# Output projection of a gated-parallel layer by Strassen's method: seven half-size products in place of eight

## The chip, the cores and the metric

One core of one Trainium2 chip runs the whole kernel. The metric is the device time of one execution in microseconds (us), the median over several runs; a profile is one further execution, recorded by the hardware profiler.

## The reference, cut to what matters

One layer over 1024 latent tokens of width 1024, with 256 context tokens: a modulated RMSNorm, one wide input projection, two branches (gated linear attention and differential attention), a gated merge, an output projection, a gate and a residual. The change touches the last three lines.

```python
def combine(o_gla, gla_gate, o_diff, diff_gate, m_gla, m_diff,
            gla_gain, diff_gain, lam_init, w_br_gla, w_br_diff, w_out):
    a = merge_heads(rms_norm(o_gla) * gla_gain) * jax.nn.silu(gla_gate)
    b = merge_heads(rms_norm(o_diff) * diff_gain * (1 - lam_init)) * jax.nn.silu(diff_gate)
    y = jax.nn.sigmoid(m_gla) * (a @ w_br_gla) + jax.nn.sigmoid(m_diff) * (b @ w_br_diff)
    return y @ w_out
...
        x = x + g_x * out_x
```

Everything is float32, y and w_out are 1024x1024.

## The kernel before, in words

All large products are done on TensorE (PE) in a split form: a float32 tensor is written as hi + lo, both in the type fp32r, and a product is three matmuls (hi by hi, hi by lo, lo by hi; `mm3`, L325). The split (`split`, L335) is a copy with rounding on ScalarE (ACT), hi, and a subtraction on VectorE (DVE), lo = source - hi. A half is thus ready when VectorE has written lo.

The order of every engine's instructions is written out when the program is built. Generators (`load`, `conv`, `half_tile`, `post_y` and so on) stand for strands of work; a `Driver` (L57) keeps a rough clock of each engine and resumes a strand when what it waits for is due by that clock. What a strand issues is appended to the queue of its engine, and on the chip each queue runs strictly in that order, waiting on semaphores for true dependences. `d.on("DVE", tile)` waits until the tile is due and the engine's queue is short; `acq` and `rel` count the buffers of a tag, and a strand that finds none waits. All DMAs go out from one queue, SP's (`dma`, L275), in the order in which they are issued.

The stages are: adaLN and input projection (phase A), both branches (phase B), and the merge and output (phase C). Beside the attention of phase B, `fill` (L1626) runs products that depend on little: gate products, the product with w_br_gla, and at the end that with w_br_diff (kind 2). For each of 8 column tiles `dt` of 128 channels and each `half` of 512 tokens, 8 x 3 matmuls make a PSUM tile `mc` [128 channels, 512 tokens]; `load_y` (L1814) brings the gate and the first branch, `post_y` (L1825) makes y on VectorE in two instructions (PSUM tile by gate, plus first branch), and splits y at once into the tag `yy`. y is thus kept transposed, channels on partitions. The right operands of `fill` sit in 32 buffers of the tag `h`, released half by half when the last product has read them.

`to_c` (L1848) opens phase C's pools and calls `wstream`, which loads w_out in 8 pieces of 512 KB (`raw`) and splits them into `h` buffers. `stream` (L1884) does the projection: for each of two column halves c of w_out and each of 8 tiles i of 128 tokens, 8 x 3 matmuls over the channel tiles k into one `mc` tile. `post_out` (L1874) finishes a tile in two VectorE instructions (PSUM tile by gate `gb`, plus x) and stores it. Four `o` buffers carry x in and the result out; `load_x` (L1867) fills them.

The seam is the moment at which PE goes from the last half-tile of y to the first tile of the projection.

## Time and profile before

| | |
|---|---|
| median of 3 runs | 1734.94 us (1734.45 to 1736.46) |
| the profiled execution: its own time | 1732.79 us |
| its span, first to last instruction | 1731.1 us |
| mean granted TensorE clock | 0.996 |
| PE busy, share of the span | 97% |
| DVE, ACT, POOL busy | 60%, 43%, 41% |

How to read the rows: PE is TensorE's matmuls and PEld its weight loads, DVE is VectorE, ACT is ScalarE, POOL is GpSimd, SP is the queue that issues the DMAs. A row of the timeline gives start and duration in us, the engine, the line of kernel.py, the operation, output<-inputs by the program's names without buffer numbers, the shapes, how many like instructions are merged (x4) and, in brackets, how long the engine had been idle and what ended that. Many operations are recorded under the line of a helper (L185 for ACT, DVE and POOL, L320 for matmuls, L285 for DMAs), so the tile names tell them apart. Rows of groups give busy time and the mean ns of one. Rows of stretches give, for a stretch in us from the span's start, the busy time of each engine with its number of instructions.

### The profile page before, as it was taken

What the parts mean: (1) busy time and instruction counts of PE and PEld (TensorE: products, weight loads), DVE (VectorE), ACT (ScalarE), POOL (GpSimd) and SP (SyncE); (2) the same over time, 40 slices, a digit from 0 to 9 for tenths busy, and PEclk for the clock granted to TensorE, in tenths of its full rate; (3) what the DMA queues carried; (4) which work ended last, traced back from release to release, by engine and by line L of the source; (5) the groups of instructions that cost most, each with busy time, mean ns of one, the idle gap of its engine ahead of it and who ended that gap; (6) DMA issues with size and microseconds to landing.
All of it is one profiled execution on the core that took longest, in us unless ns stands there. A gap on an engine that the chain in (4) does not pass through costs nothing.

```text
span 1731.1 us, 25030 instructions
## 1 busy us (share of the span) xinstructions
PE 1681.9 (97%) x8605; PEld 1398.8 (81%) x8605; DVE 1036.4 (60%) x1897; ACT 750.7 (43%) x1741; POOL 708.7 (41%) x917
## 2 busy tenths in 40 slices
PE   8999999999999999999999999999999999999998
PEld 3788788888888888888888777878878788888887
DVE  4534325525564767768653888778777787524532
ACT  4636422321343343344343666666666666522200
POOL 1500002404234345545430667777777787820000
PEclk9999999999999999999999999999999999999999
DMA  8423345453742646346345235335347652278322
GB/s 313 153 89 122 140 149 161 134 179 103 247 157 87 211 133 190 121 134 203 118 132 169 76 96 157 106 99 148 96 140 235 193 157 92 90 237 292 138 100 85
DMA packets 244751, 258.84 MB, mean 150 GB/s; under 512 B 20840, under 2 KB 176400, under 8 KB 244624
## 3 DMA queue, kind: packets, MB, share of 16 engines
q1 hardware_dynamic: 244624, 257.25, 47.2%
q8 instruction: 68, 1.11, 0.3%
q14 instruction: 59, 0.48, 0.1%
HBM read 170.68 MB, written 86.51 MB: 149 GB/s over the span
## 4 chain that ended last, share of the span: by engine, by line
PE 87%; DVE 5%; DMA 2%; ACT 2%; issue 2%; POOL 2%; SPq 0%; ACTq 0%; DVEq 0%; POOLq 0%
PE mm L320 42%; PE mc L320 12%; PE mb L320 7%; PE b L320 6%; PE s L320 5%; PE b L332 3%; DVE sm L185 3%; PE go L320 3%; PE gs L320 2%; PE gt L320 2%; PE tp L332 2%; PE st L320 2%; POOL at L185 1%; DMA w<-in_w_ada 1%; DVE e L185 1%
## 5 line engine op out<-in xcount | busy, mean ns | idle before, releaser
L320 PE MATMUL mm<-w,h 128*128 128x512 f32 x2304 | 569.3, 399 | 1.4 <-DVE w L185 1.4
L320 PEld LDWEIGHTS mm<-w,h 128*128 128x128 f32 x2304 | 425.6, 188 | 87.5 <-DVE w L185 2.1
L185 POOL TENSOR_TENSOR at<-ac,at 128x512 fp32r<-128x512 f32 (+1 forms) x192 | 222.1, 1157 | 16.0
L320 PE MATMUL mb<-h,wt 128*128 128x512 f32 x792 | 218.1, 405 | 1.2 <-ACT ft L185 0.7
L185 POOL TENSOR_SCALAR at<-ac 128x512 fp32r<-128x512 f32 (+1 forms) x192 | 145.2, 756 | 143.1 <-ACT ac L185 131.1
L185 ACT ACTIVATE p<-mm 128x512 f32<-128x512 f32 (+1 forms) x116 | 67.5, 587 | 217.3 <-PE mm L320 197.6
L320 PEld LDWEIGHTS mb<-h,wt 128*128 128x128 f32 x792 | 138.8, 189 | 25.0 <-DVE ft L185 1.5
L185 DVE TENSOR_REDUCE sm<-s 128x1 f32<-128x1024 f32 x128 | 155.6, 1216 | 3.5 <-PE s L320 2.4
L185 ACT ACTIVATE ac<-b 128x512 f32<-128x512 f32 (+1 forms) x213 | 107.9, 508 | 103.4 <-PE b L332 82.7
L320 PE MATMUL mm<-h,w 128*128 128x512 f32 x576 | 143.3, 401 | 0.7 <-DVE h L185 0.6
L185 ACT ACTIVATE e<-s,sm 128x1024 f32<-128x1024 f32 x128 | 142.7, 1115 | 0.0
L320 PE MATMUL s<-kk,aq 128*128 128x512 f32 x512 | 134.9, 397 | 0.2 <-ACT p L185 0.2
L320 PE MATMUL b<-at,vv 128*128 128x256 f32 x960 | 131.8, 287 | 3.1 <-ACT ac L185 3.1
L185 POOL TENSOR_SCALAR sm<-sm 128x1 f32<-128x1 f32 (+1 forms) x78 | 16.9, 216 | 287.4 <-DVE sm L185 167.0
L320 PEld LDWEIGHTS b<-at,vv 128*128 128x128 f32 x960 | 124.1, 192 | 7.4 <-ACT ac L185 3.9
L320 PEld LDWEIGHTS mm<-h,w 128*128 128x128 f32 x576 | 107.9, 191 | 24.1 <-DVE h L185 1.6
L185 DVE TENSOR_TENSOR w<-raw,w 128x512 fp32r<-128x512 f32 x120 | 86.3, 736 | 64.4 <-ACT w L185 63.1
L332 PE MATMUL b<-ident,e 128*128 128x128 f32 x604 | 94.2, 275 | 23.8 <-ACT ac L185 12.7
L185 POOL TENSOR_TENSOR sm<-sm,nhalf 128x1 f32<-128x1 f32 (+2 forms) x110 | 107.2, 975 | 13.9 <-DVE sm L185 7.4
L332 PEld LDWEIGHTS b<-ident,e 128*128 128x128 f32 x604 | 71.5, 140 | 44.8 <-ACT ac L185 18.7
L320 PEld LDWEIGHTS s<-kk,aq 128*128 128x128 f32 x512 | 90.8, 190 | 14.8 <-ACT p L185 0.4
L185 DVE SCALAR_TENSOR_TENSOR e<-e,sm,e 128x1280 f32<-128x1280 f32 x64 | 101.7, 1589 | 0.2
(199 smaller groups left out, 2609.4 us busy)
## 6 DMA issues: line engine op xcount, KB each, us to landing
raw<-in_w_in SPq DMA_DIRECT2D x72, 512.0 KB, 4.2
aq<-d_qT SPq DMA_DIRECT2D x128, 128.0 KB, 3.1
d_kT<-pl SPq DMA_DIRECT2D x40, 256.0 KB, 2.3
d_dv<-pl SPq DMA_DIRECT2D x40, 256.0 KB, 2.6
kk<-d_kT SPq DMA_DIRECT2D x32, 320.0 KB, 5.3
gv<-d_v SPq DMA_DIRECT2D x40, 256.0 KB, 2.8
vv<-d_dv SPq DMA_DIRECT2D x16, 640.0 KB, 6.1
d_aT<-gpl SPq DMA_DIRECT2D x64, 128.0 KB, 1.9
```

The lines of the kernel that those rows point to most:

```text
L185: f(out, *args, **kw)
L320: self.nc.tensor.matmul(out, lhsT, rhs, start=start, stop=stop)
L332: self.nc.tensor.transpose(out, src, self.ident[:n, :n])
```

## The change

The projection y @ w_out is cut into 2 x 2 blocks of 512x512. With y11..y22 (token half, channel half) and w11..w22, Strassen's method in Winograd's form makes seven block products out of sums of blocks:

- left operands, in this order: y11, y12, s1 = y21 + y22, s2 = s1 - y11, s3 = y11 - y21, y22, s4 = y12 - s2
- right operands: w11, w21, t1 = w12 - w11, t2 = w22 - t1, t3 = w22 - w12, t4 = w21 - t2, w22
- the output blocks are sums of the products: block 11 is the first two (accumulated in one PSUM tile); block 22 is the first, third, fourth and fifth; block 21 is the first, fourth, fifth and sixth; block 12 is the first, third, fourth and seventh.

Each product is 4 token tiles x 4 channel tiles x 3 matmuls, so 48 matmuls; there are 336 in place of 384. `post_y` leaves y as float32 in the tag `yf`; `left` makes the sums s1 to s4 on POOL and `right` the differences t1 to t4 on VectorE, both in float32, and each operand is split afterwards (`operand`: hi on ACT, lo on VectorE). `right` loads w11 and w21 as before into `raw`, and all four blocks again as 16 tiles into the buffers `h1`. `stream` runs the seven products in order, four token tiles each; what has to be kept of a product is drained from PSUM into the buffers `wt` and `wx` (`after`). `finish` ends the blocks 11, 22 and 21: one VectorE instruction that reads PSUM, then on POOL the product with the gate (blocks 22 and 21) and the sum with x, then the store. For block 12, `with_x` prepares gate times the earlier products plus x on POOL, and `finish12` does two VectorE instructions and the store.

To make room, the tag `h` (32) is split in two, `h0` and `h1` (16 each), for the two token halves, `kk` gets a pool of its own that is closed when phase C opens, and there are three more PSUM tiles `mz`.

```diff
-        h=("sb", 32), raw=("sb", 3), gb=("sb", 1), sm=("sb", 32), kk=("sb", 3),
+        h0=("sb", 16), h1=("sb", 16), raw=("sb", 3), gb=("sb", 1), sm=("sb", 32), kk=("sbK", 3),
...
-        yy=("sbC", 32), o=("sbC", 4), wx=("sbC", 4),
+        yy=("sbC", 24), yf=("sbC", 16), sf=("sbC", 2), o=("sbC", 4), wx=("sbC", 4),
...
-        mb=("psW", 1), s2=("psB", 2), st=("psB1", 1), b1=("psB1", 2), mc=("psC", 4),
+        mb=("psW", 1), s2=("psB", 2), st=("psB1", 1), b1=("psB1", 2), mc=("psC", 4), mz=("psD", 3),
...
-    def mm(self, out, lhsT, rhs, start, stop):
-        self.nc.tensor.matmul(out, lhsT, rhs, start=start, stop=stop)
+    def mm(self, out, lhsT, rhs, start, stop, more=False):
+        self.nc.tensor.matmul(out, lhsT, rhs, start=start, stop=stop, skip_group_check=more)
...
-    def mm3(self, out, sh, sl, mh, ml, first, last):
-        self.mm(out, sh, mh, first, False)
-        self.mm(out, sh, ml, False, False)
-        return self.mm(out, sl, mh, False, last)
+    def mm3(self, out, sh, sl, mh, ml, first, last, more=False):
+        self.mm(out, sh, mh, first, False, more)
+        self.mm(out, sh, ml, False, False, more)
+        return self.mm(out, sl, mh, False, last, more)
...
-                yield from self.acq("h", 2)
+                yield from self.acq(f"h{half}", 2)
...
-            hi = self.t("hc" if ctx else "h", [P, n], F32R)
-            lo = self.t("hc" if ctx else "h", [P, n], F32R)
+            hi = self.t("hc" if ctx else f"h{half}", [P, n], F32R)
+            lo = self.t("hc" if ctx else f"h{half}", [P, n], F32R)
...
-                        yield from self.acq("h")
-                        tt = r[j][k][half] = self.t("h", [P, 512], F32R)
+                        yield from self.acq(f"h{half}")
+                        tt = r[j][k][half] = self.t(f"h{half}", [P, 512], F32R)
...
-                    self.rel("h", e, 2 * NK)
+                    self.rel(f"h{half}", e, 2 * NK)
...
-        self.dve.tensor_tensor(my[:, 0], my[:, 0], my[:, 1], ALU.add)
-        hi = self.t("yy", [P, 512], F32R)
-        lo = self.t("yy", [P, 512], F32R)
-        self.y[dt, half] = (hi, lo)
-        yield self.d.when(my)
-        e = yield from self.split(my[:, 0], hi, lo)
+        y = self.y[dt, half] = self.t("yf", [P, 512])
+        e = self.dve.tensor_tensor(y, my[:, 0], my[:, 1], ALU.add)
...
-            yield from self.idle("st", "b1", "e5", "b1k", "aq", "vv", "at4", "at2", "ac")
-            self.close("psB1", "sbB2", "sbB")
-            self.open("sbC")
+            yield from self.idle("st", "b1", "e5", "b1k", "aq", "kk", "vv", "at4", "at2", "ac")
+            self.close("psB1", "sbB2", "sbB", "sbK")
+            self.open("sbC", "psD")
...
-            wd = self.wstream([(wo, 0), (wo, 512)], "h")
+            d.spawn(left(), prio=-2)
+            d.spawn(right(), prio=-2)
...
-            d.spawn(stream(wd, self.gb), prio=9)
-        ev_x = {(c, i): Event() for c in range(2) for i in range(8)}
+            d.spawn(stream(), prio=9)
+        LEFT = ("y11", "y12", "s1", "s2", "s3", "y22", "s4")
+        RIGHT = ("w11", "w21", "t1", "t2", "t3", "t4", "w22")
+        ev_l, ev_r = ({(n, k): Event() for n in names for k in range(4)} for names in (LEFT, RIGHT))
+        def operand(ev, tag, src, then=()):
+            hi = self.t(tag, [P, 512], F32R)
+            lo = self.t(tag, [P, 512], F32R)
+            ev.w = (hi, lo)
+            def run():
+                yield d.on("ACT", src)
+                e = yield from self.split(src, hi, lo)
+                d.set(ev, e)
+                for f in then:
+                    f(e)
+            d.spawn(run(), prio=-2)
+        def left():
+            y = lambda r, c, k: self.y[4 * c + k, r]
+            ready = {"y11": ((0, 0),), "y12": ((0, 1),), "s1": ((1, 0), (1, 1))}
+            add = self.pool.tensor_tensor
+            for n in LEFT:
+                for k in range(4):
+                    for r, c in ready.get(n, ()):
+                        yield self.ev_y[4 * c + k, r]
+                    then = ()
+                    if n in ("s1", "s2"):
+                        yield from self.acq("sf")
+                        src = self.t("sf", [P, 512])
+                        yield d.on("POOL", y(1, 0, k), y(1, 1, k))
+                        if n == "s2":
+                            add(src, y(1, 1, k), y(0, 0, k), ALU.subtract)
+                            add(src, src, y(1, 0, k), ALU.add)
+                            add(y(0, 1, k), y(0, 1, k), src, ALU.subtract)
+                        else:
+                            add(src, y(1, 0, k), y(1, 1, k), ALU.add)
+                        then = [lambda e: self.rel("sf", e)]
+                    else:
+                        src = y(*{"y11": (0, 0), "y12": (0, 1), "s3": (1, 0), "y22": (1, 1), "s4": (0, 1)}[n], k)
+                    if n == "s3":
+                        yield d.on("POOL", src)
+                        add(src, y(0, 0, k), src, ALU.subtract)
+                    yield from self.acq("yy", 2)
+                    operand(ev_l[n, k], "yy", src, then)
+        def right():
+            for n, r in (("w11", 0), ("w21", 512)):
+                for kk in range(2):
+                    yield from self.acq("raw")
+                    raw = self.t("raw", [P, 2, 512])
+                    self.dma(raw, wo[r + kk * 256:r + kk * 256 + 256, 0:512].rearrange("(k p) c -> p k c", p=P))
+                    for j in range(2):
+                        yield from self.acq("h0", 2)
+                        operand(ev_r[n, 2 * kk + j], "h0", raw[:, j], [lambda e: self.rel("raw", e)] if j else ())
+            w = {}
+            for n in ("w11", "w12", "w22", "w21"):
+                for k in range(4):
+                    yield from self.acq("h1")
+                    x = w[n, k] = self.t("h1", [P, 512])
+                    r, c = (int(n[1]) - 1) * 512 + k * P, (int(n[2]) - 1) * 512
+                    self.dma(x, wo[r:r + P, c:c + 512])
+            for n, out, a, b, last in (("t1", "w11", "w12", "w11", None), ("t2", "w11", "w22", "w11", "t1"),
+                                       ("t3", "w12", "w22", "w12", None), ("t4", "w21", "w21", "w11", None),
+                                       ("w22", "w22", None, None, None)):
+                for k in range(4):
+                    if last:
+                        yield ev_r[last, k]
+                    if a:
+                        yield d.on("DVE", w[a, k], w[b, k])
+                        self.dve.tensor_tensor(w[out, k], w[a, k], w[b, k], ALU.subtract)
+                    if k % 2:
+                        for kk in (k - 1, k):
+                            yield from self.acq("h0", 2)
+                            operand(ev_r[n, kk], "h0", w[out, kk])
+        ev_w = [Event() for _ in range(4)]
+        ev_x = {(r, c, t): Event() for r, c in ((0, 0), (1, 1), (1, 0)) for t in range(4)}
         def load_x():
-            for c, i in ev_x:
+            for r, c, t in ev_x:
...
-                xo = ev_x[c, i].t_ = self.t("o", [P, 2, 512])
+                xo = ev_x[r, c, t].t_ = self.t("o", [P, 2, 512])
+                i = 4 * r + t
...
-                d.set(ev_x[c, i])
-        def post_out(i, pm, c, gb):
-            rows, cols = slice(i * P, (i + 1) * P), slice(c * 512, (c + 1) * 512)
-            yield ev_x[c, i]
-            xo = ev_x[c, i].t_
-            e = self.dve.tensor_tensor(xo[:, 1], pm, gb[:, c], ALU.mult)
-            self.rel("mc", e)
-            yield d.when(xo)
-            self.dve.tensor_tensor(xo[:, 1], xo[:, 1], xo[:, 0], ALU.add)
-            self.store([(self.out[0, rows, cols], xo[:, 1])], ("o", 1))
-        def stream(wd, gb):
-            for c in range(2):
-                def mms(pm, i, k, wh, wl):
-                    yh, yl = self.y[k, i // 4]
-                    s = i % 4
-                    return self.mm3(pm, yh[:, s * P:(s + 1) * P], yl[:, s * P:(s + 1) * P], wh, wl, k == 0, k == NK - 1)
-                yield from self.job(wd, c, list(range(8)), lambda i, k: [self.ev_y[k, i // 4]], mms,
-                                    lambda i, pm, c=c: post_out(i, pm, c, gb), "h", "mc", last=2 - c)
+                d.set(ev_x[r, c, t])
+        def finish(r, c, t, pm, tg=None, more=None):
+            yield ev_x[r, c, t]
+            xo = ev_x[r, c, t].t_
+            gb = self.gb[:, c]
+            if more is None:
+                e = self.dve.tensor_tensor(xo[:, 1], pm, gb, ALU.mult)
+            else:
+                e = self.dve.tensor_tensor(xo[:, 1], pm, more, ALU.add)
+            if tg:
+                self.rel(tg, e)
+            def rest():
+                if more is not None:
+                    self.pool.tensor_tensor(xo[:, 1], xo[:, 1], gb, ALU.mult)
+                yield d.on("POOL", xo)
+                self.pool.tensor_tensor(xo[:, 1], xo[:, 1], xo[:, 0], ALU.add)
+                i = 4 * r + t
+                self.store([(self.out[0, i * P:(i + 1) * P, c * 512:(c + 1) * 512], xo[:, 1])], ("o", 1))
+            d.spawn(rest(), On(e, "POOL"), prio=1)
+        def with_x(t, w):
+            if t % 2 == 0:
+                yield from self.acq("raw")
+                ev_w[t].t_ = self.t("raw", [P, 2, 512])
+            x = ev_w[t].x = ev_w[t - t % 2].t_[:, t % 2]
+            self.dma(x, a["x"][0, t * P:(t + 1) * P, 512:])
+            self.pool.tensor_tensor(w, w, self.gb[:, 1], ALU.mult)
+            yield d.on("POOL", x)
+            self.pool.tensor_tensor(w, w, x, ALU.add)
+            d.set(ev_w[t])
+        def finish12(t, pm, tg, w):
+            yield ev_w[t]
+            o = ev_w[t].x
+            e = self.dve.tensor_tensor(o, pm, self.gb[:, 1], ALU.mult)
+            self.rel(tg, e)
+            yield d.on("DVE", o)
+            self.dve.tensor_tensor(o, o, w, ALU.add)
+            self.store([(self.out[0, t * P:(t + 1) * P, 512:], o)])
+        def stream():
+            Z = ("mz", "mz", "mz", "mb")
+            X, tmp = [None] * 4, {}
+            def temp(n, t):
+                if t % 2 == 0:
+                    tg = "wx" if n == "w" else "wt"
+                    yield from self.acq(tg)
+                    tmp[n, t] = self.t(tg, [P, 2, 512])
+                return tmp[n, t - t % 2][:, t % 2]
+            def after(n, t, pm, tg):
+                if n == 0:
+                    o = tmp[1, t] = yield from temp("p1", t)
+                    yield self.act.activation(o, pm, AF.Copy)
+                elif n == 1:
+                    yield from finish(0, 0, t, pm, tg)
+                elif n == 2:
+                    o = tmp[2, t] = yield from temp("v", t)
+                    self.rel(tg, self.dve.tensor_tensor(o, pm, tmp[1, t], ALU.add))
+                elif n == 3:
+                    o = tmp[3, t] = yield from temp("w", t)
+                    self.dve.tensor_tensor(o, pm, tmp[2, t], ALU.add)
+                    d.spawn(with_x(t, o), prio=1)
+                elif n == 4:
+                    yield from finish(1, 1, t, pm, None, tmp[2, t])
+                elif n == 5:
+                    yield from finish(1, 0, t, pm, tg, tmp[1, t])
+                else:
+                    yield from finish12(t, pm, tg, tmp[3, t])
+            for n in range(7):
+                for t in range(4):
+                    tg = Z[t] if n in (2, 6) else "mc"
+                    if n in (0, 2, 3, 6):
+                        yield from self.acq(tg)
+                        X[t] = self.t(tg, [P, 512])
+                    pm = X[t]
+                    for k in range(4):
+                        yield ev_l[LEFT[n], k]
+                        yield ev_r[RIGHT[n], k]
+                        (lh, ll), (rh, rl) = ev_l[LEFT[n], k].w, ev_r[RIGHT[n], k].w
+                        cs = slice(t * P, (t + 1) * P)
+                        e = self.mm3(pm, lh[:, cs], ll[:, cs], rh, rl, k == 0 and n in (0, 2, 3, 6), k == 3,
+                                     n in (1, 4, 5))
+                        yield AtPE(0)
+                        if t == 3:
+                            self.rel("yy", e, 2)
+                            self.rel("h0", e, 2)
+                    d.spawn(after(n, t, pm, tg), d.when(pm), prio=-2)
```

More of the change, by code (lines that the diff above doesn't have):

```diff
@@ L353, in build @@
                 self.t("edge", [P, self.EDGE // 4])
-                self.open("sb", "sbA", "psA", "psA1", "sbA1")
+                self.open("sb", "sbK", "sbA", "psA", "psA1", "sbA1")
                 self.phase_a()
@@ L358, in build @@
                 self.d.run()
-                self.close("psC", "psW", "sbW", "sbC", "sb", "sbE")
+                self.close("psC", "psW", "psD", "sbW", "sbC", "sb", "sbE")
     def scratch(self):
```

4 lines of the change are left out of this document (2 added, 2 removed).

## The prediction, made before the changed kernel was run

> **What bounds the kernel now.** I read the page's head first, then the chain of waits over the last 230 us, then the timeline around the seam where the last half-tile of y ends and the output projection begins, then the busy times of that stretch.
>
> ```profile
> span 1731.1 us, 25030 instructions
> ...
> 1553.49 173.26 PE mc L320 x763
> 1726.75 0.02 issue
> 1726.78 0.70 DVE o L185
> 1727.48 0.02 issue
> 1727.50 0.69 DVE o L185
> ```
>
> The chain says that from 1553.49 to 1726.75 nothing but matmuls sets the end: 173.26 us for 763 of them, 0.227 us each (each is recorded longer, because they are pipelined; the pitch is what counts). After the last one come two VectorE instructions and a store.
>
> ```profile
> 1639.54 10.81 PE L320 MATMUL mc<-h,yy 128*128 128x512 f32 x47
> 1728.22 0.33 SPq L285 DMA_DIRECT2D out_dram<-o  x1
> 1639.50:1731.10 91.60, 87.24 (x385) 71.89 (x384) 28.74 (x43) 3.87 (x7) 0.00 (x0) 1.00 0.26 95
> ```
>
> The first row is the seam, 1639.54. The last row's columns are PE, PEld, DVE, ACT, POOL, granted clock, DMA share and GB/s: the projection is 384 matmuls without a gap (87.2 us) at full clock, VectorE a third busy, POOL idle. From seam to end: 91.6 us.
>
> **The change, part by part.** *Up to the seam* the built program issues the same work in the same order: PE's first 6745 rows, ACT's 1313, DVE's 1656, POOL's 883 and SP's 837 are the same apart from buffer names. The split of the h buffers in two and the kk tiles' own pool therefore cost nothing there. The y half-tiles that follow lose the split of y (to run later) and keep their matmuls.
>
> *Removed:* one product of eight. 2 x 8 x 8 x 3 = 384 matmuls become 7 x 4 x 4 x 3 = 336; 48 x 0.227 = 10.9 us, all of it on the path. A product lasts 48 x 0.227 = 10.9 us. Without new stalls PE would end 76.3 us after the seam and the kernel would take 10.9 us less.
>
> *Added work around PE.* After the seam the built order holds on POOL 46 two-tensor operations of 128x512 f32 (s1's last two, 12 for s2 and s4, 4 for s3, 4 + 8 + 8 for three quarters of the output, 8 for the fourth's base; the first starts just before the seam), where there were none; on VectorE 83, of which 58 read both operands from SBUF (the low halves of the splits, the differences of w_out blocks, the last adds) and 25 read one operand from PSUM.
>
> ```profile
> 1646.52 2.49 DVE L185 TENSOR_TENSOR h<-raw,h 128x512 fp32r<-128x512 f32 x4
> 80.86 2.53 POOL L185 TENSOR_TENSOR rope<-rope,gains 128x512 f32<-128x512 f32 x2
> L185 POOL TENSOR_TENSOR p<-p,sm 128x512 f32<-128x512 f32 x36 | 39.7, 1104 | 2.1
> ```
>
> A VectorE operation costs 0.62 us back to back, so 83 are 52 us of some 78: by itself that fits. A POOL operation on two full tensors takes 1.27 to 1.29 undisturbed (the rope row; the third row is a cheaper form, with a broadcast scalar). 46 x 1.28 = 59 us: by itself that fits too. ACT gets about 40 splits and copies of 0.6 us and is no bound. The 4 MB of w_out in 16 pieces go out from about 5 us before the seam; at the 307 GB/s that the trace shows with the DMA engines 91% busy (the row stands with the tail, below) that is 14 us, and the third product needs the first half of them at 21.8: hidden.
>
> *The cost that the two shares hide.* These rows show POOL and VectorE at the same time:
>
> ```profile
> 325.56 1.04 POOL L185 TENSOR_TENSOR p<-p,sm 128x512 f32<-128x512 f32 x1
> 325.58 1.57 DVE L185 TENSOR_TENSOR w<-raw,w 128x512 fp32r<-128x512 f32 x1
> ...
> 684.11 0.72 DVE L185 TENSOR_TENSOR w<-raw,w 128x512 fp32r<-128x512 f32 x1
> 684.25 1.48 POOL L185 TENSOR_TENSOR p<-p,sm 128x512 f32<-128x512 f32 x1
> 684.99 1.28 DVE L185 TENSOR_TENSOR w<-raw,w 128x512 fp32r<-128x512 f32 x1 [0.16 <-ACT w L185]
> ...
> 703.04 1.29 POOL L185 TENSOR_TENSOR p<-p,gdif 128x512 f32<-128x512 f32 x1
> 703.07 0.69 DVE L185 TENSOR_TENSOR pl<-tp,pl 128x512 fp32r<-128x512 f32 x1 [0.97 <-ACT pl L185]
> ```
>
> At 325.56 POOL starts first; the VectorE subtraction of two SBUF tensors, 0.69 alone, takes 1.57 and ends 0.55 after POOL's end (327.15 against 326.60). At 684.11 VectorE starts first; POOL takes 1.48 instead of 1.04 and ends 0.90 after VectorE's end, then the next VectorE operation waits for POOL. At 703.04 the VectorE operation reads one operand from PSUM (tp) and is not delayed at all. So a VectorE instruction with two SBUF operands and a POOL instruction exclude each other and take turns; about 0.14 us at the head of each is all that overlaps. A pair of a split and a POOL add takes 0.55 + (1.285 - 0.14) = 1.69 us, and a VectorE instruction that is caught by one loses 1.69 - 0.62 = 1.07 us. The old projection had no such pair, the new one is full of them: 58 x 0.55 + 46 x 1.14 = 84 us of turns, against the 76 us that PE needs. That is why I do not credit the 10.9 us.
>
> *Walk through VectorE's queue* (us after the seam; instructions stand in the order of the built program and none can pass another). The fourth product needs the low half of t2, the fifth that of t3, the sixth that of t4, each by nine matmuls (2.0 us) after its start.
> - t1: VectorE has its last low half done at 21.9, PE wants it at 23.8: no stall, with little to spare.
> - t2: from the y drain at 1.5, VectorE has 33 instructions up to t2's last low half: 33 x 0.62 = 20.5, some 2.4 of waits for ACT and POOL, and, since POOL stands with 21 operations in a row (s1's last, s2/s4, s3, four output adds) over just this stretch, 17 full catches, 18.2 us. It ends at 42.7. PE wants it at 3 x 10.9 + 2.0 = 34.7: a stall of 8.0.
> - t3: 17 more instructions, 10.5, and 3 catches, 3.2 (POOL only gets single operations between drains here): 56.5. PE wants it at 43.6 + 2.0 + 8.0 = 53.6: 2.9.
> - t4: 16 more, 9.9, and 6 catches' worth, 6.2: 72.7. PE wants it at 54.5 + 2.0 + 10.9 = 67.4: 5.3.
> PE stalls 16 us and ends at 92 instead of 76.3.
>
> *The tail.* The third quarter of the output now goes VectorE, POOL, POOL, store; the last one VectorE, VectorE, store.
>
> ```profile
> o<-in_x SPq DMA_DIRECT2D x16, 256.0 KB, 2.6
> out_dram<-o SPq DMA_DIRECT2D x16, 256.0 KB, 2.0
> ...
> 1550.00:1600.00 50.00, 49.23 (x216) 40.14 (x215) 23.27 (x31) 11.09 (x14) 0.00 (x0) 1.00 0.91 307
> ```
>
> On SP's queue three loads of x for the third quarter stand behind the store of its first tile, which waits for POOL. POOL gets the last input of the second quarter at 77.3 and has six operations to that store: 77.3 + 6 x 1.285 + 0.5 = 85.5. Issue and landing of x, waiting for two loads' issue and the traffic, 3.7: 89.2. Then five POOL operations, two of them caught: 96.5. Behind the store of that tile SP holds the four of the last quarter, whose VectorE work ended at 94.1: five stores of 262 KB, 4.3 us at 307 GB/s and some 2 us to issue and land: 102.8 (the end before took 2.9 us from the last VectorE operation to the span's end, 1728.2 to 1731.1, with one store).
>
> **Sum.** 102.8 against 91.6: +11.2 us. Span 1639.5 + 102.8 = 1742.3; the profiled execution has 1.7 us around its span (1732.79 against 1731.1), so 1744.0. The median of the runs shown is 1734.94, 2.15 above the profiled one: I predict **1746**.
>
> *Ends of the unknown.* The trace of before shows no stretch with both queues full for 30 us. If a full catch cost 0.8 us instead of 1.07 (a POOL add at the 1.04 of the p<-p,sm form) the same walk ends at about the old time; if nothing overlapped, at 112 (below). PE's clock is a smaller open point:
>
> ```profile
> 1150.00:1153.00 3.00, 1.24 (x8) 0.70 (x6) 2.07 (x5) 1.98 (x5) 2.88 (x2) 1.00 0.56 180
> 1153.00:1157.00 4.00, 3.26 (x13) 3.07 (x14) 0.73 (x2) 2.91 (x7) 3.83 (x6) 0.58 0.11 41
> ```
>
> After 3 us in which PE was busy for 1.24, the granted clock fell to 0.58 of full over the next 4 us. The stalls of 8.0 and 5.3 us can do that, at 1.7 us for 3.4 us at half clock; but PE then waits for VectorE anyway, and between 0 and 3 us remain, of which I take 0.
>
> **The rivals.**
> *A, the saved product comes through.* VectorE and POOL find enough gaps, and all sums lie behind PE. For it: each engine's own share is under 75%, the operands have a product's time of lead. It decides at the first deadline: 34.7 - 1.5 - 2.4 - 20.5 = 10.3 us for 17 catches, 0.6 us each. Below that t2 is in time and PE never stalls: 1734.9 - 10.9 = 1724. Against it: every caught row above costs about as much as the other engine's remaining time (0.88 at 325.58 for a POOL operation of only 1.04). That the change does not remove the matmuls is excluded, since the built order has 336.
>
> *B, a draw.* The catches cost 0.8: the page calls POOL's spans rough, and waits that are recorded as busy may be partly its own. t2 is done 17 x 0.27 = 4.6 us earlier, t3 and t4 by 0.8 and 1.6 more, the tail's eleven POOL operations save 0.25 each and 0.8 on catches: 102.8 - 10.6 = 92.2 against 91.6, so 1735.5.
>
> *C, no overlap at all.* The turns last the full recorded lengths, 0.69 + 1.285 = 1.97 a pair, a catch costs 1.35. Then t2 is 17 x 0.28 = 4.8 us later still, t3 and t4 2.5 more together, the tail's POOL operations some 2: 112 after the seam, +20.5, 1755. Against it: 0.55 and 0.90 in the rows above are both about 0.14 short of the full lengths. The Trainium skill (SBUF — State Buffer, section Who interferes with whom) says that a VectorE instruction with two SBUF inputs and a GpSimd instruction that reads SBUF contend for one shared port pair, and that the first to issue holds it for the whole instruction. By its rule the sum would be that of C; in who waits and who does not, the rows agree with it, in the length they come 0.28 us a pair lower, and I go by the rows. (GpSimd is POOL in the profile.)
>
> **How the numbers follow.** The forecast with its own spread (POOL adds of 1.2 to 1.4 us, stores and loads of the tail 2 us either way: +5 to +17, so 1740 to 1752) has 0.70; A 0.12, B 0.07, C 0.11. Faster by over 0.2% (3.5 us, about what a measurement of this kernel can tell from no change): A, 0.12. Within: B, 0.07. Slower: 0.81. The range takes in B and C and leaves out A: 1734 to 1757.
>
> **What would show it.** In the profile after: PE's share of the stretch after the seam well under 100%, with its stalls on low halves (h0 from VectorE) at the start of the fourth, fifth and sixth product; none in the first three; VectorE subtractions of 1.5 to 1.75 us beside POOL adds of 1.6 to 1.7, while drains from PSUM stay at 0.69; the last stores behind POOL. I am wrong if the caught rows are not there (A), if PE stalls earlier (loads of w_out or t1 late), or if the span before the seam moves, for which I found no reason.

## The result: 1744.07 us, and the profile after

The changed kernel takes 1744.07 us (median of 6 runs, 1741.63 to 1745.79) against 1735.17 for the kernel before on the same chip: ratio 1.0047, 95% interval 1.0032 to 1.0061. The forecast was 1746, range 1734 to 1757. So the change makes the kernel slower by 0.5%, with one matmul in eight of the projection gone. The profiled execution took 1742.41 us, its span 1740.7.

The timeline of PE in the changed kernel from the seam on (bracket: idle time before the row and what ended it):

```profile
1640.77 21.92 PE L320 MATMUL mc<-h,yy 128*128 128x512 f32 x96
1662.53 8.32 PE L320 MATMUL mz<-h,yy 128*128 128x512 f32 x36
1670.69 2.88 PE L320 MATMUL mb<-h,yy 128*128 128x512 f32 x12
1673.41 1.52 PE L320 MATMUL mc<-h,yy 128*128 128x512 f32 x6
1677.14 0.50 PE L320 MATMUL mc<-h,yy 128*128 128x512 f32 x1 [2.21 <-ACT h L185]
1682.23 24.08 PE L320 MATMUL mc<-h,yy 128*128 128x512 f32 x95 [4.59 <-DVE h L185]
1707.90 0.50 PE L320 MATMUL mc<-h,yy 128*128 128x512 f32 x1 [1.59 <-ACT h L185]
1710.12 0.97 PE L320 MATMUL mc<-h,yy 128*128 128x512 f32 x3 [1.72 <-DVE h L185]
1711.81 11.68 PE L320 MATMUL mc<-h,yy 128*128 128x512 f32 x38 [0.73 <-DVE h L185]
```

Three products run without a gap. The fourth has done 6 matmuls when it stops for the third tile of t2 (first ACT's high half, then VectorE's low half), the sixth stops for t4 in the same way; the fifth does not stop. The stalls sum to 10.84 us. Two rows are also longer than their matmuls: 95 at 0.227 are 21.6 us and took 24.1, 38 are 8.6 and took 11.7. The stretches say why; their column after POOL is the granted clock:

```profile
1660.00:1673.00 13.00, 13.00 (x59) 10.74 (x58) 13.00 (x13) 4.25 (x7) 12.33 (x8) 1.00 0.00 1
...
1683.00:1690.00 7.00, 7.00 (x24) 5.56 (x23) 7.00 (x13) 1.44 (x3) 1.13 (x1) 0.71 0.14 45
...
1707.00:1716.00 9.00, 5.66 (x14) 3.99 (x15) 9.00 (x10) 3.34 (x6) 6.71 (x4) 0.72 0.08 31
...
1640.70:1740.70 100.00, 82.83 (x338) 66.27 (x336) 83.09 (x86) 24.13 (x41) 71.44 (x45) 0.92 0.31 112
```

Behind each stall the clock is near 0.7. The first row points to the cause of the stalls: VectorE busy for 13.00 of 13 us, and yet only 13 instructions done, beside 8 of POOL. Over the whole stretch (last row) 86 VectorE instructions fill 83 us, 0.97 each, where 0.62 is their pace alone.

From the seam to the end it is 99.9 us against 91.6. The ledger: 48 matmuls less, -10.9; stalls, +10.8; slower matmuls, +6.4 (the last matmul ends 93.6 after the seam, 17.3 later than 336 x 0.227 = 76.3; 5.6 of the 6.4 are in the two long rows, the rest in the short rows between the stalls); the end after the last matmul, 6.3 in place of 4.4, +2.0. Sum +8.3. The seam itself lies 1.2 us later than in the profile of before, from differences at the start and in attention; the order of the instructions there is the same.

Executions differ by some us before the seam (see the last section), so the table compares profiles from the seam on, one of each kernel, and medians beside them. Each ratio is against the kernel before, timed beside that kernel on the same chip (medians of before: 1735.2 to 1736.3 us). Chips differ from group to group of kernels, so kernels are better compared by ratio, and where two intervals overlap the times alone don't tell the kernels apart.

| kernel | seam to last matmul | seam to end | PE's stalls | median | ratio to before, 95% |
|---|---|---|---|---|---|
| before | 87.2 | 91.6 | 0 | 1735.17 | |
| changed | 93.6 | 99.9 | 10.8 | 1744.07 | 1.0047 (1.0032 to 1.0061) |
| POOL reads nothing | 76.3 | 85.1 | 0 | 1729.07 | 0.9961 (0.9944 to 0.9979) |
| POOL reads one tensor at a time | 80.2 | 90.5 | 1.9 | 1734.29 | 0.9988 (0.9976 to 1.0000) |
| all sums on VectorE | 84.8 | 95.6 | 5.3 | 1740.29 | 1.0021 (1.0009 to 1.0033) |
| finishing on VectorE | 84.3 | 99.1 | 4.7 | 1743.27 | 1.0036 (1.0025 to 1.0048) |
| all on VectorE, ordered | 91.6 | 97.5 | 9.6 | 1740.37 | 1.0031 (1.0020 to 1.0043) |
| POOL in half turns | 84.7 | 96.8 | 5.4 | 1740.74 | 1.0027 (1.0017 to 1.0037) |
| PE's stalls filled | 90.9 | 98.4 | | 1741.92 | 1.0034 (1.0021 to 1.0047) |
| prepared, high rank | 76.3 | 80.3 | 0 | 1732.83 | 0.9985 (0.9972 to 0.9997) |
| prepared, low rank | 76.3 | 79.9 | 0 | 1736.32 | 1.0001 (0.9987 to 1.0015) |
| prepared, three split late | 80.7 | 84.3 | 2.7 | 1736.59 | 1.0003 (0.9993 to 1.0014) |
| prepared, two split late | 77.8 | 81.4 | 1.2 | 1738.41 | 1.0012 (1.0001 to 1.0024) |

### The profile page after: what moved, and what is told of

It is laid out like the page before. It is cut to its first block, busy times and chain, and to the rows that moved or that the text cites. A ratio compares the mean times of both kernels' runs of the same rounds, so it can differ in the third digit from the quotient of the medians.

```text
span 1740.7 us, 25110 instructions
## 1 busy us (share of the span) xinstructions
PE 1677.0 (96%) x8557; PEld 1391.7 (80%) x8557; DVE 1088.1 (63%) x1933; ACT 767.4 (44%) x1769; POOL 784.9 (45%) x965
## 4 chain that ended last, share of the span: by engine, by line
PE 83%; DVE 8%; ACT 3%; DMA 2%; issue 2%; POOL 2%; SPq 1%; ACTq 0%; DVEq 0%; POOLq 0%
PE mm L320 41%; PE mc L320 9%; PE mb L320 8%; PE b L320 6%; PE s L320 5%; PE b L332 3%; DVE sm L185 3%; PE go L320 3%; PE gs L320 2%; PE gt L320 2%; PE tp L332 2%; PE st L320 2%; DVE h L185 1%; POOL at L185 1%; DMA w<-in_w_ada 1%
```

## The experiments

### Does POOL hold VectorE up because it reads SBUF?

```diff
+    def pw(self, out, a, b, op):
+        self.pool.tensor_tensor(out[:, :1], a[:, :1], b[:, :1], op)
+        self.pool.memset(out[:, 1:], 0.5)
+        return self.pool.memset(out[:, 1:384], 0.5)
-            add = self.pool.tensor_tensor
+            add = self.pw
...
-                self.pool.tensor_tensor(xo[:, 1], xo[:, 1], xo[:, 0], ALU.add)
+                self.pw(xo[:, 1], xo[:, 1], xo[:, 0], ALU.add)
```

> Every POOL addition, subtraction and multiplication of the new projection is replaced by one of a single column and two memsets that keep POOL busy about as long but read nothing (so the sums s1 to s4, the gate and x are left out of the result; counts, waits, buffers and the order of every queue stay). Theory 1, exclusion (a VectorE instruction with two SBUF operands and a POOL instruction that reads SBUF take turns): VectorE's subtractions go back to 0.62 to 0.7 us, t2 is done 1.5 + 2.4 + 33 x 0.62 = 24.4 us after the seam, ahead of the 34.7 at which PE wants it, PE has no stall, its clock stays at full, and it ends 76.3 us after the seam; with a tail of 5 to 6 us the end is at 81 to 83 and the time 1725 to 1727. Rival, lateness: the stalls come because POOL has a long queue and delivers its sums late, whatever it reads. Then the stalls at the fourth and sixth product stay, seam to end stays near 100, and the time near 1744.

Measured: 1729.07 us, no stall, the last matmul 76.3 us after the seam, the end at 85.1. The groups of VectorE in the projection, first of the changed kernel, then of this one, and this one's POOL (busy time, then mean ns of one):

```profile
L185 DVE TENSOR_TENSOR h<-h,h 128x512 fp32r<-128x512 f32 x20 | 24.4, 1244 | 0.0
L185 DVE TENSOR_TENSOR h<-h,h 128x512 f32<-128x512 f32 x16 | 22.1, 1393 | 0.0
...
L185 DVE TENSOR_TENSOR o<-mc,wt 128x512 f32<-128x512 f32 x8 | 5.5, 683 | 5.1 <-DMA out_dram<-o 5.1
```

```profile
L185 DVE TENSOR_TENSOR h<-h,h 128x512 fp32r<-128x512 f32 x20 | 13.4, 684 | 0.0
L185 DVE TENSOR_TENSOR h<-h,h 128x512 f32<-128x512 f32 x16 | 10.5, 684 | 0.0
```

```profile
L185 POOL MEMSET o<- 128x511 f32 x20 | 10.5, 524 | 0.0
L185 POOL MEMSET o<- 128x383 f32 x20 | 8.4, 419 | 1.1
...
L185 POOL TENSOR_TENSOR o<-o 128x1 f32<-128x1 f32 x12 | 3.0, 253 | 1.2 <-DMA o<-in_x 1.2
```

The same VectorE instructions fall from 1244 and 1393 ns to 684, while POOL is occupied for 0.25 + 0.52 + 0.42 = 1.2 us per operation, nearly as long as an undisturbed sum (1.28), and reads only one column. The drain that reads PSUM had 683 all along. Lateness falls as a rival: in the changed kernel VectorE waits for another engine's result for only some 2.3 us between the seam and t2; the rest of its delay is in instructions that last longer. What stalls PE is that POOL and VectorE both read SBUF. End and time came 2 to 4 us above what I gave: the tail is 8.8 us after the last matmul, where POOL now has three instructions per operation ahead of the last stores.

### Is POOL any help, then?

```diff
-            add = self.pool.tensor_tensor
+            add = self.dve.tensor_tensor
...
-                self.pool.tensor_tensor(xo[:, 1], xo[:, 1], xo[:, 0], ALU.add)
+                self.dve.tensor_tensor(xo[:, 1], xo[:, 1], xo[:, 0], ALU.add)
```

> All 46 POOL operations of the new projection go to VectorE; the same computation. VectorE then has 129 instructions after the seam in place of 83, POOL none. Theory 1, exclusion: none is caught any more, so 129 x 0.62 = 80 us with a few us of waits, seam to end 92 to 97, the time 1736 to 1741, that is 3 to 8 us less than the changed kernel though VectorE gets 46 instructions more. Rival, POOL is real help and each catch costs only a little: then the 46 x 0.62 = 28.5 us come on top of a VectorE queue that already makes PE wait, and the time rises by 10 to 28 us to 1754 or more.

> Only the 28 POOL operations of the output's finishing (gate and x) go to VectorE; the sums s1 to s4 stay on POOL. Theory 1: s2 and s3 still catch VectorE up to t2, so the stall at the fourth product stays (4 to 7 us); the tail loses POOL's operations and the two late catches. Seam to end 95 to 99, time 1739 to 1743, between the changed kernel and the one with all on VectorE. Rival, POOL is real help: 28 x 0.62 = 17 us more on VectorE, slower than the changed kernel by 5 us or more.

Measured: 1740.29, in the range of theory 1, and 1743.27, 0.3 above it; both rivals, 1754 and 5 us above the changed kernel, fall. By the ratios the first is faster than the changed kernel (1.0009 to 1.0033 against 1.0032 to 1.0061, all but apart), the second can't be told from it. (In both, two tiles of the third quarter of the output were read from PSUM only after the next product had been added, so that quarter is another sum.) The stretch from seam to end with all sums on VectorE:

```profile
1640.70:1736.30 95.60, 79.56 (x337) 63.38 (x335) 81.18 (x131) 24.66 (x42) 0.00 (x0) 0.94 0.33 116
```

Beside 83.09 us for 86 instructions above: VectorE does 45 instructions more in 2 us less. POOL's 71 us of work were worth nothing to VectorE. With only the finishing moved, the fourth product's stall is 4.7 in place of 6.8 and the sixth has none (no POOL sum is left there), but the gain goes into the tail: 99.1 - 84.3 = 14.8 us of finishing after the last matmul.

Since the order had moved as well, a second kernel held it:

```diff
+                    if n in (1, 4, 5):
+                        yield drained[n - 1, t]
...
-            d.spawn(rest(), On(e, "DVE"), prio=1)
+            d.spawn(rest(), On(e, "DVE"), prio=-3)
```

> All 46 POOL operations on VectorE again, with two changes of order: PE begins the next product in a PSUM bank only after the bank has been read (in the first such run VectorE read two tiles of the third quarter of the output only after the next product had been added to them, so that quarter was another sum), and the finishing of the output goes ahead of the splits. Theory 1: VectorE alone sets the pace, 129 x 0.62 = 80 us and its waits; 95 to 100 us from the seam, stalls of 5 to 11 us on PE, the time 1738 to 1743, a little under the changed kernel. Rival: the 1740 of the first run came only from the drains that stood late in VectorE's queue; in their right place the time is at or above the 1744 of the changed kernel.

Measured: 1740.37, 97.5 us from the seam, stalls 9.6, as theory 1 said. The median is under the 1744.07 of the changed kernel, but the intervals overlap (1.0020 to 1.0043 against 1.0032 to 1.0061), so the times alone do not exclude the rival. What is shown is that taking 46 operations from POOL costs this kernel nothing. VectorE alone, 129 x 0.62 = 80 us, does not fit beside 76 us of PE without stalls, though. Where the work is placed only trades PE's stalls (5.3 or 9.6) against the tail (10.8 or 5.9).

### What does the clock cost?

```diff
+            FILL = {(3, 2, 0): 8, (3, 2, 1): 17, (5, 2, 0): 6, (5, 2, 1): 6, (5, 3, 1): 2}
...
+            zero = self.t("zz", [P, P], F32R)
+            yield self.act.activation(zero, self.gb[:, 0, :P], AF.Copy, scale=0.0)
```

> At the places where the changed kernel's PE stood still (the start of the fourth and the sixth product) it gets 39 more matmuls with a zero stationary operand, about 0.23 us each, that add nothing to the sums: 8 + 17 in stalls of 2.2 + 4.6 us, 6 + 6 + 2 in 1.6 + 1.7 + 0.7 us. Nothing else is changed. Theory, the clock: the half clock behind each stall costs time of its own, about 2.5 us behind the first and 3 to 4 behind the second (95 matmuls took 24.1 us in place of 21.6, the next 38 took 11.7 in place of 8.6). With PE kept busy the granted clock stays near 1.00, the second part at least comes back, and all of it if VectorE keeps pace: 1744 - 3 to 1744 - 6.4, so 1738 to 1741. Rival: the clock's loss is only PE waiting for VectorE in another form; then the stalls grow by what the matmuls gain, and the time stays within 1 us of 1744.

Measured: 1741.92, 0.9 above the range of the theory and 2.1 below the rival's 1744; in ratios 1.0034 against 1.0047, with intervals that overlap, so the answer is read from the profiles behind the seam. PE's timeline around the fourth to sixth product, and two stretches:

```profile
1681.17 1.98 PE L2036 MATMUL mc<-h,zz 128*128 128x512 f32 x8
1683.56 0.50 PE L320 MATMUL mc<-h,yy 128*128 128x512 f32 x1 [0.41 <-ACT h L185]
1683.89 4.08 PE L2036 MATMUL mc<-h,zz 128*128 128x512 f32 x17
1688.69 12.19 PE L320 MATMUL mc<-h,yy 128*128 128x512 f32 x51 [0.72 <-DVE h L185]
1702.21 10.55 PE L320 MATMUL mc<-h,yy 128*128 128x512 f32 x44 [1.34 <-DVE h L185]
1712.60 1.56 PE L2036 MATMUL mc<-h,zz 128*128 128x512 f32 x6
...
1718.32 8.92 PE L320 MATMUL mc<-h,yy 128*128 128x512 f32 x38 [0.27 <-DVE h L185]
```

```profile
1687.00:1713.00 26.00, 23.92 (x102) 18.45 (x101) 26.00 (x32) 8.51 (x15) 14.02 (x8) 1.00 0.10 33
1713.00:1722.00 9.00, 8.17 (x33) 5.74 (x33) 9.00 (x9) 3.35 (x6) 6.88 (x5) 1.00 0.08 30
```

The clock stays at 1.00 and both answers are half right. Behind the *first* stall the recovered time is lost again: a stall of 1.34 appears at t3 (1702.21), which the slow clock had covered, and the wait for t4 ends 1718.32 - 1647.17 = 71.15 us after the seam as against 1711.81 - 1640.77 = 71.04. VectorE sets that moment, whatever PE does. Behind the *second* no wait follows, and 38 matmuls take 8.92 in place of 11.68: 2.76 us, which the last matmul keeps (90.9 against 93.6). The end keeps 1.5 of them (98.4 against 99.9).

### Does the length of POOL's turn matter?

```diff
+    def pw(self, out, a, b, op):
+        self.pool.tensor_scalar(out, a, 1.0, 0.0, ALU.mult, ALU.add)
+        return self.pool.tensor_scalar(out, b, 1.0, 0.0, ALU.mult, ALU.add)
```

> As in the run whose POOL reads nothing, every POOL operation of two tensors in the new projection is replaced, here by two POOL operations that each read one tensor of 128x512 and write one (0.62 us alone in the gb row of the kernel before, so about as long together; the sums, the gate and x are again left out). It asks whether one read is enough to shut VectorE out, and whether the length of POOL's turns matters. Theory, turns of whole instructions for any POOL instruction that reads SBUF: VectorE's two-SBUF subtractions are caught again, but by turns of 0.62 in place of 1.28, so about 0.68 + 0.5 = 1.1 to 1.2 us when caught; with both queues full the pair of a subtraction and two POOL operations still takes about 1.7 to 1.9 us for one or two subtractions, so t2 comes earlier than in the changed kernel: stalls of 0 to 6 us in place of 10.8, time 1731 to 1741. Rival 1: only two-tensor POOL operations exclude VectorE; then it is like the run without reads, 1729. Rival 2: what counts is POOL's whole time with reads; then as the changed kernel, 1744.

```diff
+    def pw(self, out, a, b, op):
+        n = out.free_size() // 2
+        for i in range(2):
+            s = slice(i * n, (i + 1) * n)
+            e = self.pool.tensor_tensor(out[:, s], a[:, s], b[:, s], op)
+        return e
```

> The changed kernel with each POOL operation of the new projection issued as two of 128x256 in place of one of 128x512; the same sums by the same engine. Theory, turns of whole instructions: a VectorE subtraction that is caught loses the rest of a turn of some 0.75 us (the 128x256 rows of the kernel before have 0.73 to 0.78) in place of 1.28, so about 1.1 to 1.15 us in place of 1.7; VectorE gains about 0.5 on each of 17 catches up to t2, the stalls at the fourth product go from 6.8 us to 0 to 2, those at the sixth stay partly. POOL pays: 92 instructions, each waiting for a VectorE instruction, so its adds come later and the tail grows by 1 to 4 us. Seam to end 90 to 97 (the run with one read per POOL instruction had 90.5), time 1734 to 1741. Rival: the port's total time counts, not the length of a turn; halves cost more of it (92 x 0.75 = 69 in place of 59 us), so the stalls grow and the time is 1745 to 1755.

Measured: 1734.29 and 1740.74. One group of VectorE with one read per POOL instruction; then of the half turns the same group, POOL's costliest one, and PE's first stall:

```profile
L185 DVE TENSOR_TENSOR h<-h,h 128x512 fp32r<-128x512 f32 x20 | 19.3, 989 | 0.0
```

```profile
L185 DVE TENSOR_TENSOR h<-h,h 128x512 fp32r<-128x512 f32 x20 | 20.9, 1058 | 0.0
```

```profile
L185 POOL TENSOR_TENSOR o<-o 128x256 f32<-128x256 f32 x24 | 20.5, 887 | 0.0
```

```profile
1688.08 3.88 PE L320 MATMUL mc<-h,yy 128*128 128x512 f32 x10 [3.24 <-DVE wx L185]
```

One read is enough to shut VectorE out (989 against 684 with none), and a shorter turn costs it less (1058 against 1244). In both, the fourth product runs its 48 matmuls without a stop, the best case of what was expected; the last matmul comes 13 and 9 us earlier than in the changed kernel. With half turns the first stall moves to the fifth product, where PE waits for a drain of the fourth (wx) that stands in VectorE's queue (in this version, as in "all on VectorE, ordered", PE begins a product in a used PSUM bank only when the drain of that bank stands in VectorE's queue, which the changed kernel does not ask for). And POOL pays: 96.8 - 84.7 = 12.1 us from the last matmul to the end in place of 6.3. Over the stage VectorE is busy for 78.4 us in place of 83.1, POOL for 86.0 in place of 71.4: cutting POOL's turns up moves the loss from VectorE to POOL. By the ratio (1.0017 to 1.0037) the half turns can't be told from the changed kernel.

### A version that takes the work out of the stage

The right operands do not depend on y. Two kernels form and split them during attention (by VectorE and ACT), store the halves and only load them in the projection; with the gate multiplied into them first, the gate's instructions at the end vanish.

```diff
+        self.d.spawn(self.prep(), prio=-1)
...
+            E(x, x, self.gb[:, c], ALU.mult)
...
+            self.store([(self.d_r[i][0][k], hi), (self.d_r[i][1][k], lo)], ("pt", 2), ev=self.ev_r[n, k])
...
-                    yield from finish(1, 1, t, pm, None, tmp[2, t])
+                    e = self.dve.tensor_tensor(o, pm, tmp[2 if n == 4 else 1, t], ALU.add)
```

> The right operands (w11, w21, t1 to t4, w22) are multiplied by the gate, subtracted and split into their halves during the attention stage, by VectorE and ACT, stored to DRAM and only loaded in the projection; the gate's multiplications at the end fall away, x is added by POOL to kept products. After the seam VectorE keeps some 55 instructions and POOL 30. Theory, the shared port is what binds the projection: with about 50 instructions less there PE has no stall, 76.3 us of matmuls and 3 to 6 us of tail, 80 to 82 from the seam in place of 99.9. The price is paid in attention, where VectorE is busy for 76 to 80% and POOL for 71 to 79%: 60 VectorE instructions of 0.62 to 0.8 us over 450 us, of which a tenth to a fifth may reach PE, 4 to 9 us. Sum 1735 - 11 + 4 to 9: 1728 to 1733. Rival: attention has no room at all, and PE loses all 37 us and more of them: 1755 or above.

> The same, with the preparation at a lower rank in the order of the attention stage (it goes into the queues later than that stage's own work, in place of ahead of most of it). After the seam the same 80 to 82 us. In attention its instructions fill gaps better if the queues have gaps; if they stand in front of instructions whose input is late already, they cost more. Between 1727 and 1737.

Measured: 1732.83 and 1736.32. The stage from the seam of the first; then the stretch of attention, of the kernel before and of the first:

```profile
1653.00:1733.40 80.40, 76.38 (x337) 62.90 (x336) 33.26 (x43) 12.93 (x21) 40.22 (x29) 1.00 0.57 209
```

```profile
1000.00:1500.00 500.00, 473.31 (x2867) 408.04 (x2866) 388.84 (x693) 314.71 (x817) 372.99 (x419) 0.99 0.46 134
```

```profile
1000.00:1500.00 500.00, 471.13 (x2811) 400.18 (x2811) 441.72 (x745) 327.26 (x841) 391.08 (x410) 0.99 0.56 168
```

The projection is now what the change meant it to be: 76.4 us of matmuls, no gap, 80.3 to the end, 11.3 less than before. Attention gives most of it back: 52 VectorE instructions more fill 53 us more (a full us each, as beside a busy POOL), and PE gets 56 matmuls fewer through in the same 500 us of these two profiles. By the medians 11.3 - 3.5 = 7.8 us are lost ahead of the seam. Of the kernels that compute the layer's output the first is the only one that is faster than before (0.9985, upper end 0.9997), by a margin near the limit of what can be told. The lower rank did not help: 3.5 us more by the medians, with intervals that overlap.

Splitting some operands late was meant to relieve attention:

```diff
+            if n in self.LATE:
+                self.store([(self.d_r[self.RN.index(n)][0][k], src)], ev=self.ev_r[n, k])
+                yield self.ev_r[n, k]
+                return
```

> As the prepared versions, but t3, t4 and w22 are stored as f32 sums and split in the projection stage, where VectorE was busy for only 40%: 12 VectorE and 12 ACT instructions less in attention, 12 more behind the seam, and the lower rank of the second version. Theory: behind the seam 80.3 + 0 to 4 (POOL's adds catch some of the splits, PE does not wait): 80 to 84; in attention, where the 60 prepared instructions cost 8 to 14 us, 48 cost 5 to 9. Sum 1736 - 10 + 7: 1729 to 1735. If it is slower than the first prepared version by 3 us or more, the splits do reach PE in the projection.

> Between the two: only t4 and w22 are split late, 8 instructions moved. 1729 to 1736.

Measured: 1736.59 and 1738.41, outside what I gave. Behind the seam the splits did reach PE, by this row of the first:

```profile
1703.85 12.59 PE L320 MATMUL mc<-h,yy 128*128 128x512 f32 x48 [2.72 <-DVE o L185]
```

The sixth product cannot start in a PSUM bank before VectorE has drained it, and that drain stands behind splits that POOL's adds of x had caught (the last three took 1.74 to 1.77 us each, two of a left operand and one of those split late). That is 4.0 us more than the first prepared version from the seam on, and the median is 4.9 us further from before (+1.4 against -3.5), so attention gave nothing back that can be seen. What a VectorE instruction costs there is not settled by these four: 48, 52 and 60 of them, in other orders, cost no amounts that follow their number.

## Why the prediction was right

*Nothing changes before the seam:* held, to 1.2 us, less than executions differ by there.

*The removal, -10.9:* held; with no exclusion the last matmul is at 76.3 after the seam, the number of the prediction.

*The exclusion and its price:* held; it sets when t2, t3 and t4 are ready, and so what PE loses up to the sixth product. In the changed kernel both queues are full around 1655. Four of VectorE's subtractions of two SBUF tensors, then POOL's turns beside them (a merged row carries the types of its first instruction: two of the four are splits of t1, two are differences of w_out blocks):

```profile
1651.85 6.88 DVE L185 TENSOR_TENSOR h<-h,h 128x512 fp32r<-128x512 f32 x4
```

```profile
1651.45 1.62 POOL L185 TENSOR_TENSOR sf<-sf,yf 128x512 f32<-128x512 f32 x1
1653.15 1.62 POOL L185 TENSOR_TENSOR yf<-yf,sf 128x512 f32<-128x512 f32 x1
1654.74 1.74 POOL L185 TENSOR_TENSOR sf<-yf,yf 128x512 f32<-128x512 f32 x1
```

A turn of one and one takes 6.88 / 4 = 1.72 us, 1.70 from one POOL start to the next; predicted 1.69 from three rows of before. Rival C needed 1.97 and falls; rival A needed catches under 0.6 us and falls. The Trainium skill (SBUF — State Buffer, section Who interferes with whom) makes the loser wait for the whole instruction. On who waits, the runs agree: two SBUF inputs against a POOL instruction that reads SBUF (989 to 1393 ns), not against one that only writes (684), not with an operand from PSUM (683). On the length they stay 0.25 us a pair under the sum of the two recorded lengths.

*The walk through VectorE's queue:* t2 done at 42.7, measured 42.0 (the stall ends at 41.5, with its third tile); t3 at 56.5, measured 54.9; t4 at 72.7, measured 71.0. Up to t2 the trace has the 33 instructions of the walk, 15 caught for a full turn and 4 for a part, which costs 18.2 us, and 2.3 us of waits; the walk had 17 catches for 18.2 and 2.4. That is no luck of the sum: its terms came out one by one. (One slip: a low half is wanted after ten matmuls of its product, not nine: the sixth product's last stop comes after 6 + 1 + 3; 0.2 us.)

*PE's stalls:* the walk has 8.0, 2.9 and 5.3, together 16.2, which put PE's end at 92.5 (the text rounds to 92). The changed kernel has 6.8, none at the fifth product, and 4.0, together 10.8. With the clock held they are 7.3 (from 1681.17 to 1688.69, less one matmul), 1.3, and 4.8 (from 1712.60 to 1718.32, less four). PE ends at 93.6 all the same, since it waits for t4 either way: t4 came 1.7 earlier than in the walk, and the clock took 2.8 behind it.

*The clock, "between 0 and 3 us remain, of which I take 0":* a term of the wrong size. The reason given (PE then waits for VectorE anyway) holds for the first stall, where 2.5 us of slow matmuls replace a stall of 1.3 at t3 and part of the one at t4. Behind the last stall there is nothing left to wait for, and it cost PE 2.8 us, 1.5 of them at the end of the kernel. The rule for the point: slow matmuls behind a stall cost nothing only if another wait for the same queue follows.

*The tail, from PE's end at 92 to 102.8:* too long, 6.3 us measured behind the last matmul. The order is as described, with the last stores behind POOL. POOL's last rows, VectorE's last, then SP's:

```profile
1727.63 1.29 POOL L185 TENSOR_TENSOR o<-o 128x512 f32<-128x512 f32 x1 [1.96 <-DMA o<-in_x]
1728.88 3.00 POOL L185 TENSOR_TENSOR o<-o,gb 128x512 f32<-128x512 f32 x2
1731.84 2.98 POOL L185 TENSOR_TENSOR o<-o 128x512 f32<-128x512 f32 x2
```

```profile
1735.13 0.69 DVE L185 TENSOR_TENSOR raw<-raw,wx 128x512 f32<-128x512 f32 x1
```

```profile
1728.95 6.23 SPq L285 DMA_DIRECT2D out_dram<-o  x3
1735.22 2.02 SPq L285 DMA_DIRECT2D out_dram<-raw  x4
```

POOL is done at 1734.82, 94.1 after the seam (96.5 in the walk), and SP needed 2.0 us for the last four issues and 3.5 to the end where I gave 4.3 for five transfers and 2 more. PE's own end did not set this: VectorE has the last tile done at 1735.82, but its store is the last of four issues of some 0.5 us each that go out behind POOL's last store, and leaves about 0.9 us later. So 102.8 became 99.9, 2.4 us by POOL's walk and some 0.5 by the stores; the seam lay 1.2 later, and the 1746 was 2 us high. Range, direction and mechanism held.

## What to carry to other kernels

Before giving POOL a share of VectorE's work, price it on the port that they share: here a POOL sum took 1.1 us (1.72 - 0.62) out of a busy VectorE that would have done it in 0.62, and moving all of it back cost nothing (by the ratios 2.8 to 4.5 us less, the first within what can't be told). The rows leave POOL as help beside VectorE instructions that read PSUM (683 ns, undisturbed), or where VectorE is idle; where both must read SBUF, shorter POOL instructions shifted the loss from VectorE to POOL's own deadlines. Removing an eighth of the matmuls only pays if the sums that replace them fit the stage, or can be formed in another stage that has room.

## What the runs showed of the hardware that was not expected

A PE that waits can hold its clock: with 39 matmuls by zero in the stalls the granted clock stayed at 1.00 where it had been 0.71 and 0.72, for 2.8 us of PE's time at the last of them. The executions agree: their mean clock is 0.993 to 0.997, the changed kernel's 0.990 to 0.993. The Trainium skill (TensorE: Matmul & The Clock Gate, Part 1) describes such a gate, half rate after an idle window of about 3.4 us. The stall of 4.6 us fits it. Ahead of the second drop no wait is over 1.72 us and four matmuls stand between the waits, so PE need not be idle all that time.

The clock also falls at different moments ahead of the seam, where the kernels do the same. In the first 100 us, where weights arrive, before and the run with filled stalls:

```profile
40.00:60.00 20.00, 17.50 (x76) 12.32 (x75) 15.11 (x25) 14.76 (x32) 6.84 (x13) 0.83 0.91 289
60.00:80.00 20.00, 20.00 (x113) 16.45 (x112) 11.13 (x19) 13.57 (x23) 12.51 (x24) 1.00 0.23 82
```

```profile
40.00:60.00 20.00, 17.32 (x85) 11.46 (x82) 15.16 (x25) 14.23 (x31) 6.48 (x11) 1.00 0.90 270
60.00:80.00 20.00, 16.95 (x83) 13.72 (x82) 9.65 (x14) 12.19 (x20) 10.27 (x17) 0.83 0.29 102
```

In the first the clock is low while PE also waits for data (DMA share 0.91). In the second it is low 20 us later, and PE waits there too, for 3.05 of the 20 us: 83 matmuls in place of 113. By the seam that execution is 7.6 us late, with the same matmuls in the same order. How much of that is the clock and how much late data these rows do not separate. In the 12 executions of that kernel, 1739 to 1747 us, the mean clock is 0.997 in the shortest and 0.993 in the longest, which fits a part for the clock but does not show it as the cause. Either way stages are best compared from the seam on.
